# A first tile's products by kind behind 8 warm-up products, and the first head's outputs turned through HBM

## The chip, the cores and the metric

The kernel runs on one core of one Trainium2 chip. The metric is the device time of one execution in microseconds (us), lower is better. Three runs of the kernel before gave a median of 1380.77 us (1380.72 to 1381.59).

The core has five engines with a queue of instructions each, which run in order inside a queue and beside each other between queues: TensorE (PE, with its weight loads as PEld), VectorE (DVE), ScalarE (ACT), GpSimd (POOL) and SyncE (SP, which only starts DMA transfers here).

## The reference

Two layers on 512 tokens of width 1024. Each layer projects the normed x to pool inputs, q, k, v and two gates, mixes the tokens in two ways, adds the gated sum, and ends with a SwiGLU of width 2816.

```python
xn = rmsnorm(x, norm1_g[i])
u_pool, q, k, v, g_a, g_b = split(xn @ w_in[i])
q, k = rotary(rmsnorm(q, q_norm_g)), rotary(rmsnorm(k, k_norm_g))
# 4 heads; each has two q/k pairs of 128 and a v of 256; chunk-causal mask
p = softmax(q @ k.T * 128 ** -0.5)
o = (p[0] - lam * p[1]) @ v
o = rmsnorm(o, subln_g) * (1.0 - lam_init)
merged = sigmoid(g_a) * pool_mixer(u_pool) + sigmoid(g_b) * o
x = x + merged @ w_out[i]
gate, up = split(rmsnorm(x, norm2_g[i]) @ w_ffn_in[i])
x = x + (silu(gate) * up) @ w_ffn_out[i]
```

## The kernel before

**Products.** Every matrix product is made of three: an operand is split into a high part (a cast on ScalarE, `whi`, `xh`, `qh`, `ah`) and a low part (a subtraction on VectorE, `wlo`, `xl`, `ql`, `al`), and PE adds high times high, low times high and high times low into one PSUM bank. `split` (L214 to L216) does it for weights and activations alike; `product` (L304 to L315) issues the three.

**Order.** Python code issues the instructions. Work that has to wait for another engine is put off: `later` (L264) puts a function into a heap with a due time in a clock that counts columns of products issued (512 for a product of 512 columns), and `run_due` takes out what is due between two groups of three products. The framework's scheduler then orders every queue again, so that the program's order on an engine is not that of the code; names carry a number that grows with the order of the code, and the numbers of one tile differ a little between the two programs. Each buffer comes from a pool named by its tag: `mt` and `qn` have three buffers each, and a tile waits until one is free.

**Start (L406 to L485).** PE makes warm-up products of a zeroed tile `cold` (12, L406 to L408). `first_step(0)` (L450) loads the first weight piece and the first x tile in halves, splits the weights (L216), scales x by the norm's gain into `xh` on VectorE (L472) and makes `xl` (L473). `first_products` (L477) adds the products of one k into the four banks of `first_acc`, one for each 128 tokens: three products for a bank, then the next bank.

**Heads.** Heads come in the order 3, 2, 1, 0. The first head of layer 0 is treated apart (`at_start`). For each head, `attention` (L514) projects q and k for four token blocks t = 0 to 3. `evicted` (L625) takes the squares of a block out of PSUM into `qn` (L629), `rsqrt_mean` finds the norm's factor (VectorE L355, POOL L356), ScalarE scales the block (L634), VectorE rotates it (L385 to L393), and it is turned, so that `turn` (L527) can scale (L535) and split it into `qh` and `ql` (L216). `scores` (L539) makes the scores, their maxima and exponentials (L551); `turn_prob` (L568) splits the turned probabilities into `ah` and `al`; `weighted` (L587) multiplies them by v, takes squares into `mt` (L595) and a factor `r`; `gated` (L598, its instruction L599) scales `mt` with r and the gate `tb`; `turn_out` (L609) turns `mt` and puts it, scaled, into `mj` (L618). Then v and gate `tb` of the head are projected (`vh` L676, `tb` L679 and L680).

**Two ways to turn.** `turned` (L321) turns a tile through HBM: VectorE transposes blocks of 32 by 32 into `near` (L326), SP writes `near` to HBM (`away`, L327) and reads it back in four transfers (L331). For the first head, q, k, probabilities and outputs are instead transposed by PE against an identity (L317, L318).

**Merge.** For each head, `merged` (from L683) makes the pool mixer's input `up` (L699 to L710) and the gate `ta` (VectorE L733, tanh on ScalarE L737), and multiplies the pool part by its own weights `pw`. It follows a head by one: the merge of head 3 runs while head 2 is made, that of head 2 while head 1 is made.

## Time and profile before

| | before |
|---|---|
| median of three runs | 1380.77 us (1380.72 to 1381.59) |
| the profiled execution | 1380.28 us |
| its span, first to last instruction | 1378.5 us |
| chain that ended last: PE's share | 95% |
| mean granted TensorE clock | 0.999 |
| DMA, bytes moved | 224.07 MB, 163 GB/s |

The profile records one execution. Its "span" leaves out 1.8 us around the first and last instruction. A group's row reads: line, engine, operation, output and inputs with their shapes and count, then the busy time and the mean time of one in ns, then the idle time of the engine ahead of the group and what ended it. A row of the timeline reads: start and duration in us, engine, line, operation; in brackets stands the engine's idle time ahead of it and what released it. A matmul's row lasts longer than the distance to the next one, since matmuls are pipelined; what counts is the distance of the starts.

### The profile page before, as it was taken

The page shows a single profiled execution, that of the slowest core. Times are in us where ns is not written, and L with a number is a line of the kernel's source. Part 1 is how long each engine was busy: PE and PEld are TensorE (multiplying, and loading weights), DVE is VectorE, ACT ScalarE, POOL GpSimd, SP SyncE. Part 2 cuts the span into 40 slices and gives each one's busy share as a digit, 9 for nine tenths or more (in the row PEclk, how much of TensorE's full clock was granted, in tenths as well). Part 3 has the DMA queues.
Part 4 walks back from the last instruction along what each step waited for, and adds up shares of the span by engine and source line. Part 5 has one row for each costly group of instructions (what it writes and reads, how often), then busy time and mean ns, then how long its engine had stood idle before and what let it go on. Part 6 is the DMA issues. An engine that isn't in the chain of part 4 may idle for free.

```text
span 1378.5 us, 18671 instructions
## 1 busy us (share of the span) xinstructions
PE 1371.7 (100%) x6242; PEld 1138.8 (83%) x6242; DVE 995.6 (72%) x1787; ACT 774.9 (56%) x1577; POOL 129.2 (9%) x155
## 2 busy tenths in 40 slices
PE   9999999999999999999999999999999999999999
PEld 7888888888888888888888888888888888888887
DVE  7668677676968768678666696775878687686782
ACT  7675564554856545554367655545557665555540
POOL 3010100000101101110010001000001111000100
PEclk9999999999999999999999999999999999999999
DMA  8334454545668868686435454544536788787731
GB/s 312 99 130 126 129 152 141 150 123 153 126 188 194 226 186 222 172 204 189 144 108 150 122 186 134 164 124 138 172 111 139 194 212 219 187 212 179 204 122 61
DMA packets 141072, 224.07 MB, mean 163 GB/s; under 512 B 41392, under 2 KB 88496, under 8 KB 140976
## 3 DMA queue, kind: packets, MB, share of 16 engines
q1 hardware_dynamic: 130464, 187.20, 42.5%
q0 software_dynamic: 9216, 33.56, 14.2%
q10 hardware_dynamic: 1296, 2.13, 0.6%
q8 instruction: 49, 0.80, 0.2%
q14 instruction: 47, 0.39, 0.1%
HBM read 193.59 MB, written 29.23 MB: 162 GB/s over the span
## 4 chain that ended last, share of the span: by engine, by line
PE 95%; ACT 1%; DVE 1%; issue 1%; DMA 0%; POOL 0%; SPq 0%; ACTq 0%; DVEq 0%; POOLq 0%
PE mm L293 15%; PE mm L294 14%; PE mm L292 14%; PE mm L311 14%; PE mm L313 14%; PE mm L312 14%; PE sc L292 3%; PE sc L294 3%; PE sc L293 3%; PE sc L311 1%; PE sc L312 1%; ACT whi L216 1%; PE sc L313 1%; DVE wlo L216 0%; PE mm L318 0%
## 5 line engine op out<-in xcount | busy, mean ns | idle before, releaser
L216 DVE TENSOR_TENSOR wlo<-raw,whi 128x1024 fp32r<-128x1024 f32 (+1 forms) x221 | 267.6, 1215 | 74.9 <-ACT whi L216 74.0
L216 ACT CAST whi<-raw 128x1024 fp32r<-128x1024 f32 (+1 forms) x221 | 230.3, 1050 | 145.4 <-PE mm L294 57.8
L311 PE MATMUL mm<-whi,xh 128*128 128x512 f32 x480 | 188.9, 394 | 0.0
L313 PE MATMUL mm<-whi,xl 128*128 128x512 f32 x480 | 187.2, 390 | 0.0
L312 PE MATMUL mm<-wlo,xh 128*128 128x512 f32 x480 | 187.1, 390 | 0.0
L293 PE MATMUL mm<-fl,whi 128*128 128x512 f32 (+1 forms) x356 | 137.6, 387 | 0.0
L294 PE MATMUL mm<-fh,wlo 128*128 128x512 f32 (+1 forms) x356 | 137.6, 387 | 0.0
L292 PE MATMUL mm<-fh,whi 128*128 128x512 f32 (+1 forms) x356 | 137.6, 387 | 0.0
L752 DVE TENSOR_TENSOR res<-mm,res 128x512 f32<-128x512 f32 (+1 forms) x145 | 97.7, 679 | 45.0 <-PE mm L294 41.8
L242 POOL DMA_DIRECT2D wlo<-in_wts x64 | 56.1, 876 | 536.6 <-ACT wlo L241 342.8
L313 PEld LDWEIGHTS mm<-whi,xl 128*128 128x128 f32 x480 | 90.1, 188 | 19.2
L356 POOL TENSOR_TENSOR r<-r,mhalf 128x4 f32<-128x4 f32 (+1 forms) x64 | 57.4, 898 | 516.7 <-DVE r L355 503.0
L311 PEld LDWEIGHTS mm<-whi,xh 128*128 128x128 f32 x480 | 90.2, 188 | 17.3
L312 PEld LDWEIGHTS mm<-wlo,xh 128*128 128x128 f32 x480 | 90.3, 188 | 17.2
L311 PE MATMUL mm<-xh,whi 128*128 128x512 f32 x256 | 99.8, 390 | 0.0
L312 PE MATMUL mm<-xl,whi 128*128 128x512 f32 x256 | 99.8, 390 | 0.0
L313 PE MATMUL mm<-xh,wlo 128*128 128x512 f32 x256 | 99.6, 389 | 0.0
L292 PE MATMUL mm<-whi,xh 128*128 128x512 f32 x224 | 87.1, 389 | 0.0
L293 PE MATMUL mm<-wlo,xh 128*128 128x512 f32 x224 | 87.1, 389 | 0.0
L294 PE MATMUL mm<-whi,xl 128*128 128x512 f32 x224 | 87.1, 389 | 0.0
L241 ACT ACTIVATE wlo<-raw 128x1024 fp32r<-128x1024 f32 x64 | 67.7, 1058 | 29.5 <-PE mm L293 25.7
L292 PEld LDWEIGHTS mm<-fh,whi 128*128 128x128 f32 x356 | 66.9, 188 | 13.7
(232 smaller groups left out, 2964.2 us busy)
## 6 DMA issues: line engine op xcount, KB each, us to landing
raw<-in_wts SPq DMA_DIRECT2D x243, 512.0 KB, 3.9
wlo<-in_wts POOLq DMA_DIRECT2D x64, 512.0 KB, 6.3
away<-near SPq DMA_DIRECT2D x73, 256.0 KB, 2.2
near<-away SPq DMA_DIRECT2D x292, 64.0 KB, 2.5
away<-near SPq DMA_DIRECT2D x29, 128.0 KB, 1.7
near<-away SPq DMA_DIRECT2D x116, 32.0 KB, 2.5
pwr<-in_pool_w ACTq DMA_DIRECT2D x8, 256.0 KB, 3.1
out<-res SPq DMA_DIRECT2D x7, 256.0 KB, 2.0
```

Source lines behind the costliest of these rows:

```text
L216: return nc.scalar.copy(hi, src), nc.vector.tensor_sub(lo, src, hi.bitcast(F32))
L241: made[0] = nc.scalar.activation(lo, raw, AF.Copy, scale=-1.0)
L242: nc.gpsimd.dma_start(lo.rearrange("p a b -> p (a b)"), wts[piece_no], accum_op=ALU.add)
L292: nc.tensor.matmul(acc, lhsT=ah, rhs=bh, start=start, stop=False, **check)
L293: nc.tensor.matmul(acc, lhsT=ah, rhs=bl, start=False, stop=False, **check)
L294: last = nc.tensor.matmul(acc, lhsT=al, rhs=bh, start=False, stop=stop, **check)
L311: nc.tensor.matmul(acc, lhsT=ah, rhs=bh, start=i == 0, stop=False)
L312: nc.tensor.matmul(acc, lhsT=ah, rhs=bl, start=False, stop=False)
L313: last = nc.tensor.matmul(acc, lhsT=al, rhs=bh, start=False, stop=i == n - 1)
L356: nc.gpsimd.tensor_tensor(r, r, mhalf[:, :width], op=ALU.pow)
L752: return nc.vector.tensor_add(res[d][:, cs], acc, res[d][:, cs])
```

## The change

1. `WARM` goes from 12 to 8.
2. In `first_step(0)`, for the first half, only the cast to `whi` is issued ahead; the code issues the subtraction for `wlo` behind `xh` and `xl` of the first x tile.
3. The twelve products of the first x tile are issued by kind: high by high for four token blocks, then `xl` by `whi` for four, then `xh` by `wlo` for four.
4. The outputs of the first head go through `turned`, as those of the other heads do, with the delay `MERGE_AWAY`; the two constants of the other way go. Eight PE transposes of `mt` (two for each token block) go; four VectorE transposes, four writes to HBM and sixteen read-backs come. The HBM turn takes a second buffer of the tag `mt` for `near`.

```diff
-WARM = 12
+WARM = 8
...
-SCORE_WAIT, PROB_WAIT, AV_WAIT, NORM_WAIT, MERGE_WAIT = 33600, 25200, 11400, 15000, 15000
+SCORE_WAIT, PROB_WAIT, AV_WAIT = 33600, 25200, 11400
...
-                split(hi[:, ks, :], lo[:, ks, :], wr[:, ks, :])
+                if i or ks.start:
+                    split(hi[:, ks, :], lo[:, ks, :], wr[:, ks, :])
+                else:
+                    nc.scalar.copy(hi[:, 0, :], wr[:, 0, :])
...
                 made = nc.vector.scalar_tensor_tensor(xl[:, k, :], xr[:, a, :], g, xh[:, k, :].bitcast(F32), op0=ALU.mult, op1=ALU.subtract)
+                if not k:
+                    made = nc.vector.tensor_sub(lo[:, 0, :], wr[:, 0, :], hi[:, 0, :].bitcast(F32))
...
-    for step in steps[0] + steps[1]:
+    k, wh, wl = steps[0][0]
+    for a, b in ((xh, wh), (xl, wh), (xh, wl)):
+        for t in range(NT):
+            nc.tensor.matmul(first_acc[t], lhsT=a[:, 0, token(t)], rhs=b, start=a is xh and b is wh, stop=False)
+    clock[0] += 3 * NT * 512
+    for step in steps[0][1:] + steps[1]:
...
-                    if at_start:
-                        later(MERGE_WAIT - GATED, lambda: turn_out(t, m))
-                    else:
-                        near = turned(m, 2, "mt", 3)
-                        later(MERGE_AWAY - GATED, lambda: turn_out(t, near))
+                    near = turned(m, 2, "mt", 3)
+                    later(MERGE_AWAY - GATED, lambda: turn_out(t, near))
...
-                if at_start:
-                    tp = tr_ps()
-                    for a in range(2):
-                        transpose(tp[:, a * P:(a + 1) * P], m[:, a * P:(a + 1) * P])
-                    into, src = mj[:, :, token(t)], tp[:, :VD].rearrange("p (a c) -> p a c", a=2)
-                else:
-                    into, src = squares_of(mj[:, :, token(t)]), m
+                into, src = squares_of(mj[:, :, token(t)]), m
```

The change moves instructions on the queues in three places that matter below. The new file's lines differ from the old ones by a few (L595 is now L605, L216 stays).

The first place is VectorE's queue at the start of the program; before, it reads:

```order
L703 MEMSET us 128x16 x2
L216 TENSOR_TENSOR wlo<-raw_114,whi 128x512
L472 TENSOR_SCALAR xh<-res_82,scale 128x512
L473 SCALAR_TENSOR_TENSOR xl<-res_82,scale,xh 128x512
L216 TENSOR_TENSOR wlo<-raw_114,whi 128x512
```

And with the change:

```order
L704 MEMSET us 128x16 x2
L478 TENSOR_TENSOR wlo<-raw_110,whi 128x512
L475 TENSOR_SCALAR xh<-res_82,scale 128x512
L476 SCALAR_TENSOR_TENSOR xl<-res_82,scale,xh 128x512
L216 TENSOR_TENSOR wlo<-raw_110,whi 128x512
```

The subtraction for `wlo` has a new line, but it stands where it stood: the scheduler puts it ahead of `xh` and `xl` in both programs.

The second place is ScalarE's queue in the second head (j = 2) up to `qh` of its token block t = 1, here qh_662 made from near_872, later qh_658 made from near_884. Before, from the block's scaling back some rows:

```order
L634 ACTIVATE qn_917<-mm_807,r_923 128x128
L216 CAST whi_1016<-raw_1014 128x1024
L216 CAST whi_1022<-raw_1020 128x1024
L618 ACTIVATE mj_240<-mm_961,scale_70 128x128 x2
L535 ACTIVATE near_872<-near_872,scale_70 128x2x4x32
L629 ACTIVATE qn_988,ss4_989<-mm_927 128x128
L216 CAST qh_662<-near_872 128x4x128
```

With the change, where qn_932 is the q and k of block t = 2, qn_1000 that of t = 3, near_868 the first head's output t = 1 on its way through HBM, and pr_1081 the probabilities of t = 0:

```order
L635 ACTIVATE qn_932<-mm_803,r_938 128x128 x4
L630 ACTIVATE qn_1000,ss4_1001<-mm_942 128x128 x4
L635 ACTIVATE qn_1000<-mm_942,r_1006 128x128 x4
L561 ACTIVATE pr_1081,st_1082<-sc_1084,mx_1083 128x128
L561 ACTIVATE pr_1081,st_1082<-sc_1091,mx_1083 128x128
L677 ACTIVATE vh_1010<-mm_1038,stats_249 128x256
L619 ACTIVATE mj_236<-near_868,scale_70 128x128 x2
L568 ACTIVATE rc_1098<-st_1082 128x1
L680 ACTIVATE tb_1012<-mm_1038,stats_249 128x256
L681 ACTIVATE tb_1012<-tb_1012 128x256
L545 ACTIVATE near_884<-near_884,scale_70 128x2x4x32
L216 CAST qh_658<-near_884 128x4x128
```

`qh` of t = 1 stood ahead of all but the first square of block t = 3; now the whole eviction of t = 3, the exponentials of t = 0 and the first v and gate stand ahead of it.

The third place is ScalarE's queue at the end of the second head, where `ah` (ah_1483, later ah_1494) is the cast of the last block's probabilities and `mt` (mt_1511, later mt_1527) the squares of the weighted block t = 2. Before:

```order
L216 CAST whi_1606<-raw_1604 128x1024
L737 ACTIVATE ta_1490<-ta_1490 128x512
L216 CAST ah_1483<-pr_1296 128x512
L595 ACTIVATE mt_1511,sso_1510<-mm_1500 128x256
L216 CAST whi_1612<-raw_1610 128x1024
```

With the change:

```order
L216 CAST whi_1734<-raw_1732 128x1024
L605 ACTIVATE mt_1527,sso_1526<-mm_1516 128x256
L216 CAST whi_1789<-raw_1787 128x1024
L738 ACTIVATE ta_1561<-ta_1561 128x512
L216 CAST ah_1494<-pr_1312 128x512
```

And VectorE's queue at the same place with the change:

```order
L355 TENSOR_SCALAR r_1529<-sso_1526,rc_1237 128x1
L216 TENSOR_TENSOR wlo_1735<-raw_1732,whi_1734 128x1024
L609 SCALAR_TENSOR_TENSOR mt_1527<-mm_1516,r_1529,tb_1013 128x256
L734 TENSOR_TENSOR ta_1561<-mm_1508,hg_222 128x512
L216 TENSOR_TENSOR wlo_1790<-raw_1787,whi_1789 128x1024
```

`ah` stood ahead of `mt`; now it stands behind `mt` and behind the tanh of a gate tile `ta_1561`, which VectorE makes behind `mt`'s scaling. On PE, six products of 512 columns (mm_1508, which `ta_1561` is made from) stand between the weighted products of t = 2 (mm_1516) and the first one that reads `ah` (mm_1563); before, they were 18.

## The prediction

> **What bounds the kernel now.** I read the page's span and busy times first, then PE's waits.

> ```profile
> span 1378.5 us, 18671 instructions
> PE 1371.7 (100%) x6242; PEld 1138.8 (83%) x6242; DVE 995.6 (72%) x1787; ACT 774.9 (56%) x1577; POOL 129.2 (9%) x155
> ```
> ```profile
> PE sc L311 <- ACT pr L551: 1.6, 2, 1.0
> ```

> PE is busy for the whole span, and its longest wait behind the start is 1.6 us in two pieces. So time is won only where PE gets less work or the start is shorter, and lost wherever PE is made to wait: any wait on PE is added in full. The sum is made against the profiled execution, 1380.28 us (the span and 1.8 us around it); the median of the runs lies 0.5 us above.

> **The start (edits 1 to 3).**

> ```profile
> 1.59 0.15 PEld L408 LDWEIGHTS <-cold 128*128 128x128 bf16 x1 [0.28 <-issue]
> ...
> 4.57 0.15 PEld L408 LDWEIGHTS <-cold 128*128 128x128 bf16 x1 [0.27 <-issue]
> ...
> 4.78 0.48 DVE L472 TENSOR_SCALAR xh<-res,scale 128x512 fp32r<-128x512 f32 x1
> 4.97 0.31 PEld L408 LDWEIGHTS <-cold 128*128 128x128 bf16 x2 [0.24 <-issue]
> ...
> 5.40 0.19 PEld L480 LDWEIGHTS mm<-whi,xh 128*128 128x128 f32 x1
> ...
> 6.10 0.19 PEld L482 LDWEIGHTS mm<-whi,xl 128*128 128x128 f32 x1 [0.29 <-DVE xl L473]
> ...
> 6.21 0.19 PEld L480 LDWEIGHTS mm<-whi,xh 128*128 128x128 f32 x1
> 6.44 0.40 PE L480 MATMUL mm<-whi,xh 128*128 128x512 f32 x1
> ```

> By the rows of the order, VectorE does the same things in the same sequence as before, so `xh` still ends at 4.78 + 0.48 = 5.26. The first real weight load came at 5.40, behind the last warm-ups; without those it can come at 5.26 plus one handover of about 0.06, at 5.32. The third product waited for `xl` until 6.10; issued by kind, the first product that needs `xl` is the fifth. The load at 6.10 was followed by the next at 6.21, so a product starts 0.11 behind its load, and the fourth product started at 6.44. Now it can start at 5.32 + 0.11 + 3 x 0.229 = 6.12 (0.229 is the distance of products, below). That is **0.3 us gained**, and the load for `xl`, due at 6.12, just meets it. If VectorE did `xh` first, as the code is written, some 0.6 (the `wlo` subtraction) would come on top; the order rows exclude it. No DMA of the start moves.

> The eight warm-ups end early. Loads of warm-ups follow each other at (4.57 - 1.59) / 7 = 0.426 us and from 4.97 on closer: some 3.8 us behind the first product, at 1.18 by the same timeline, the pace rises. Eight of them end at 1.59 + 7 x 0.426 = 4.57, and PE then stands idle until 5.3. Whether the pace still rises is a rival, below; I take it that it does, since the hole is 0.7 of some 4 us.

> **Eight PE transposes (edit 4, what goes).**

> ```profile
> 77.49 0.38 PE L318 MATMUL mm<-ident,mt 128*128 128x128 f32 x2
> ...
> 77.95 0.39 PE L312 MATMUL mm<-wlo,xh 128*128 128x512 f32 x1
> ...
> 80.24 0.40 PE L313 MATMUL mm<-whi,xl 128*128 128x512 f32 x1
> ```

> From 77.95 to 80.24 there are ten distances of products: 0.229 each. From 77.49 to 77.95 a pair of transposes and one product pass: the pair costs 0.46 - 0.229 = 0.23, four pairs **0.9 us gained**.

> **The HBM turn (edit 4, what comes).** VectorE gets four transposes of 0.435 (row below), 1.7 us, at 72% busy. ScalarE's `mj` copies change only their source. SP gets four writes and sixteen read-backs:

> ```profile
> 79.75 0.34 SPq L327 DMA_DIRECT2D away<-near  x1
> 81.98 1.73 SPq L331 DMA_DIRECT2D near<-away  x4
> ```

> That is 4 x 2.07 = 8.3 us of SP's queue. Weights' loads and the read-back of the second head's q and k queue behind them. I cost that at nothing: `whi` casts in this stretch wait for no load (row below), and the read-back of `near` for t = 1 has over 3 us in hand by the chain below. Otherwise each 0.1 us of lateness there would add to A.

> What costs is the new order on ScalarE and VectorE. The schedule puts other work ahead of what PE waits for.

> **A: `qh` of t = 1 in the second head.** Before:

> ```profile
> 79.98 0.28 ACT L629 ACTIVATE qn<-mm 128x128 f32<-128x128 f32 x1
> ...
> 81.00 0.64 ACT L618 ACTIVATE mj<-mm,scale 128x128 f32<-128x128 f32 x2
> ...
> 87.65 0.68 ACT L216 CAST qh<-near 128x512 fp32r<-128x512 f32 x1
> ...
> 90.72 1.15 ACT L634 ACTIVATE qn<-mm,r 128x128 f32<-128x128 f32 x4 [0.67 <-POOL r L356]
> ...
> 93.92 0.37 ACT L551 ACTIVATE pr<-sc,mx 128x128 f32<-128x128 f32 x1 [0.66 <-DVE mx L550]
> ...
> 94.28 0.50 ACT L535 ACTIVATE near<-near,scale 128x256 f32<-128x256 f32 x1
> ...
> 96.28 0.42 ACT L680 ACTIVATE tb<-tb 128x256 f32<-128x256 f32 x1
> ```
> ```profile
> 96.93 0.28 PE L311 MATMUL sc<-qh 128*128 128x256 f32 x1
> ```
> ```profile
> 84.79 0.56 DVE L385 TENSOR_TENSOR m<-qn,hg 128x128 f32<-128x128 f32 x3 [2.89 <-ACT qn L634]
> ...
> 85.71 0.71 DVE L326 STREAM_TRANSPOSE near<-qn 128x512 f32<-128x512 f32 x1
> ```
> ```profile
> L216 DVE TENSOR_TENSOR wlo<-raw,whi 128x1024 fp32r<-128x1024 f32 x12 | 14.5, 1211 | 0.8 <-ACT whi L216 0.6
> L216 ACT CAST whi<-raw 128x1024 fp32r<-128x1024 f32 x12 | 12.5, 1060 | 0.2 <-PE mm L313 0.2
> ...
> L356 POOL TENSOR_TENSOR r<-r,mhalf 128x1 f32<-128x1 f32 x8 | 4.5, 560 | 56.0 <-DVE r L355 48.3 <-DVE up L698 6.8 <-DVE m L385 0.9
> L356 POOL TENSOR_TENSOR r<-r,mhalf 128x4 f32<-128x4 f32 x4 | 4.1, 1013 | 38.1 <-DVE r L355 38.1
> ...
> L595 ACT ACTIVATE mt<-mm 128x256 f32<-128x256 f32 x8 | 3.1, 393 | 6.1 <-PE mm L313 4.7 <-PE mm L318 1.5
> ...
> L595 ACT ACTIVATION_READ_ACCUMULATOR mt<-mm 128x1 f32 x8 | 1.7, 208 | 0.0
> L355 DVE TENSOR_SCALAR r<-sso,rc 128x1 f32<-128x1 f32 x8 | 1.6, 200 | 0.0
> ...
> L326 DVE STREAM_TRANSPOSE near<-mt 128x256 f32<-128x256 f32 x3 | 1.3, 435 | 0.0
> ```

> PE's clock starts at W = 77.49, the end of the last weighted block. Before, PE read this `qh` at 96.93, 19.4 behind W, and it had been cast nine us earlier. Now PE reaches it 19.2 behind W (three more products stand ahead, +0.7; four pairs fewer, -0.9).

> ScalarE's clock starts at E, the end of the squares of block t = 2. Nine products stand behind W (8 x 0.229, the last ends 0.40 later: 2.23), then four squares (81.00 - 79.98 = 1.02) and a `qh` cast (0.63) between them: E = W + 3.9, so PE needs the cast at E + 15.3. The chain from E, in the new order: one `whi` cast 1.06, two `wlo` 2.42, the new transpose of an output 0.44, another `wlo` 1.21, `r` on VectorE 0.20, on POOL first the output's 0.56 and then the block's 1.01, scaling 1.15 (row 90.72), rotation and transpose 1.63 (84.79 to 86.42), only then the squares of t = 3, 1.02, for which `qn` has no buffer before; `r` again 1.21, scaling 1.15, two exponentials 0.74 (94.28 - 93.92 for one), two `mj` copies 0.64, and v, scale, cast, `rc` and two `tb`, all of 94.28 to 96.70, 2.42. That makes 16.9, with six handovers of 0.06 17.2: PE waits **1.9 us**. One `wlo` of 1.21 more or less in the chain bounds it: 0.7 to 3.1. The output's read-back is no part of it: sent at E + 3.9, it lands by the rows of SP's queue some 6.2 later, at E + 10.1, and ScalarE takes it at E + 13.8. Queued behind the waiting ScalarE are only v and `tb`.

> **B: `ah` of t = 3, end of the second head.**

> ```profile
> L599 DVE SCALAR_TENSOR_TENSOR mt<-mm,r,tb 128x256 f32<-128x256 f32 x7 | 3.4, 484 | 3.9 <-POOL r L356 3.9
> ...
> L733 DVE TENSOR_TENSOR ta<-mm,hg 128x512 f32<-128x512 f32 x2 | 1.4, 680 | 0.0
> L737 ACT ACTIVATE ta<-ta 128x512 f32<-128x512 f32 x2 | 1.3, 631 | 0.7 <-DVE ta L733 0.7
> ```
> ```profile
> 132.46 0.60 ACT L216 CAST ah<-pr 128x512 fp32r<-128x512 f32 x1
> ```

> Behind the weighted block t = 2 PE has six products, 1.37 us, before it needs `ah`; it had 18. The cast stands behind this chain: the drain 0.16, squares and their read 0.39 + 0.21, `r` on VectorE 0.20, a `wlo` 1.21 (longer than POOL's 0.56 beside it), `mt`'s scaling 0.48, `ta` 0.68, tanh 0.63, the cast itself 0.60: 4.56. PE waits 4.56 - 1.37 = **3.2 us**. If VectorE is ahead of its `wlo`, the chain begins with `ta`, 0.17 behind the sixth product: 1.37 + 0.17 + 0.68 + 0.63 + 0.60 - 1.37 = 2.1. If the third product also waits for `al` behind another `wlo`, 3.6. `wlo` and `whi` casts that stand between feed later products and are not waited for.

> **C and smaller ones.**

> ```profile
> 105.71 0.29 DVE L216 TENSOR_TENSOR al<-pr,ah 128x128 fp32r<-128x128 f32 x1 [0.73 <-ACT ah L216]
> ```

> Here VectorE waited for `ah` and was at hand. Now `up` of head 3 (shape of the `ta` row, 0.68) stands ahead of this `al` in VectorE's order: 0.17 + 0.68 + 0.29 = 1.14 behind the last `up` product, and PE has two products of 256 columns (0.12 each) and one of 512 in that time, 0.47: **0.7 us**, with 0 below if VectorE gets it done in a gap. For other places where scores meet a later exponential I take 0.5 (0 to 1).

> **Sum**: 1380.3 - 0.3 - 0.9 + 1.9 + 3.2 + 0.7 + 0.5 = 1385.4 for the profiled execution's kind, rounded with the 0.5 to the median 1385.8. With all terms at their low ends 1382.4, with all at their high ends 1388.0. Behind the second head the two programs run in the same order, so what is lost there stays lost.

> **Rivals.**

> 1. *The pace rises late.* If it needs an unbroken stretch like the 3.8 us of before, counted from the first real product, products of 0.426 instead of 0.229 run for 3.8 us: 3.8 x (1 - 0.229 / 0.426) = 1.8 us on top, 1387.6. For it speaks that no row shows a rise after a hole; against, that PE is busy most of the time. Chance 0.18.

> [...]

> 2. *A and C are hidden, B is not*: 1380.8 - 1.2 + 3.2 + 0.5 = 1383.3, within 0.2%. ScalarE took `qh` at 87.65, nine us ahead, and may still be early if the POOL steps overlap. Chance 0.12.

> 3. *The other side: both chains hidden.* PE never waits at A or B and only the gains are left: 1380.8 - 1.2 = 1379.6. It decides at chain A under 15.3 and B under 1.4 us. For it: ScalarE is 56% busy. Against it: B's four serial steps from `ta` on alone take 2.1 more than PE has. Chance 0.07; nearly all of it within 0.2%.

> 4. *The stalls make others behind them*, through late `mj` or merge tiles, two more of B's lower size, 4.2: 1390.0. Chance 0.06.

> 5. *The code's order holds on VectorE*: 0.6 better than any of these; the order rows are against it. Chance 0.01.

> **How the numbers follow.** The forecast, A, B and C paid and the pace as before, has 0.56. 0.2% of the time, 2.8 us, is about what a measurement can tell from no change: slower begins at 1383.5, faster at 1378.0. The forecast and rivals 1 and 4 are slower, all but a tail of the forecast near 1383: 0.79. Rivals 2, 3 and the tail are within: 0.18. Faster: 0.03. The range 1382.4 to 1388.8 holds the forecast's bounds, most of rival 1 and 2, and leaves out 3 and 4.

> **What would show it.** In the start: the first real load at 5.32, the fourth product at 6.12 and no wait for `xl`; distances of 0.43 behind 5.3 would mean rival 1. No L318 rows of `mt`. Among PE's waits, one of about 2 us for ScalarE's `qh` (or `near`) near 97 us, one of about 3 us for `ah` near 140, one of 0.7 for VectorE's `al` near 117. From 145 us on each group of products should lie later by one constant amount, about 5. I am wrong if PE's waits sum to under 2 us there, if they lie elsewhere, or if weights' loads come late behind the new transfers on SP's queue.

## The result and the profile after

| | before | after |
|---|---|---|
| median of six runs | 1380.88 us | 1387.92 us (1387.29 to 1388.90) |
| the profiled execution | 1380.28 us | 1387.48 us |
| its span | 1378.5 us | 1385.6 us |
| chain that ended last: PE's share | 95% | 92% |

The changed kernel takes 1.0051 times as long, with an interval of 1.0041 to 1.0061: 7.0 us more. The forecast was 1385.8, slower, in a range of 1382.4 to 1388.8.

The page's first lines and PE's waits of the changed kernel:

```profile
span 1385.6 us, 18681 instructions
PE 1373.3 (99%) x6230; PEld 1138.4 (82%) x6230; DVE 997.8 (72%) x1791; ACT 775.8 (56%) x1577; POOL 130.4 (9%) x155
```
```profile
PE mm L311 <- ACT ah L216: 3.4, 2, 3.2
PE sc L311 <- ACT pr L561: 1.6, 2, 1.0
PE sc L311 <- ACT qh L216: 1.5, 1, 1.5
...
PE mm L313 <- DVE al L216: 0.5, 1, 0.5
PE mm L494 <- DVE xh L475: 0.5, 1, 0.5
```

The three forecast waits are there: `ah` 3.2 (B), `qh` 1.5 (A), `al` 0.5 (C). The wait on the exponentials was there before. But the waits' sum is not what the time rose by, and PE's busy time has grown by 1.6 us, though PE does less work. The timeline of PE shows it behind wait B:

```profile
137.66 0.39 PE L313 MATMUL mm<-xh,wlo 128*128 128x512 f32 x1
141.29 0.38 PE L311 MATMUL mm<-vh,ah 128*128 128x256 f32 x1 [3.24 <-ACT ah L216]
...
142.33 0.34 PE L313 MATMUL mm<-vh,al 128*128 128x256 f32 x1
142.47 0.42 PE L311 MATMUL mm<-vh,ah 128*128 128x256 f32 x1
142.68 0.41 PE L312 MATMUL mm<-vl,ah 128*128 128x256 f32 x1
...
145.24 0.63 PE L313 MATMUL mm<-uh,pw 128*128 128x512 f32 x1
145.67 0.46 PE L311 MATMUL mm<-uh,pw 128*128 128x512 f32 x1
145.97 0.40 PE L312 MATMUL mm<-ul,pw 128*128 128x512 f32 x1
```

Until 142.3 products follow each other as always; from 142.47 on, a product of 256 columns takes 0.213 instead of 0.118 and one of 512 columns 0.427 (145.24 to 145.67) instead of 0.227; from 145.97 on the old pace is back. The windows say why; the columns are the window, its sum, busy times and counts of PE, PEld, DVE, ACT and POOL, then the granted clock, the DMA share and GB/s:

```profile
141.30:142.30 1.00, 1.00 (x5) 0.89 (x6) 0.66 (x1) 0.53 (x2) 0.00 (x0) 1.00 0.00 0
142.30:145.90 3.60, 3.60 (x15) 3.28 (x14) 0.00 (x0) 0.00 (x0) 0.00 (x0) 0.53 0.00 0
145.90:150.00 4.10, 4.10 (x19) 3.35 (x19) 4.09 (x8) 2.01 (x6) 0.55 (x1) 1.00 0.46 116
```

The granted clock is 0.53 over 3.6 us, right behind a wait of 3.2 us; the trace's own record of it has 0.5 from 142.39 to 145.80, 3.4 us. In these 3.4 us PE gets (1 - 0.227 / 0.427) x 3.4 = 1.6 us less done. The span's rise of 7.1 us, by its terms:

| term | forecast | measured in the profile |
|---|---|---|
| start | -0.3 | +0.2: the squares of the first head's block t = 2 begin at 62.61, 62.40 before |
| eight PE transposes | -0.9 | -0.9 (taken over: they are gone) |
| A, `qh` at 97 | 1.9 | 1.7 |
| B, `ah` at 140 | 3.2 | 3.4 (141.29 - 137.66 less one product) |
| C, `al` at 117 | 0.7 | 0.7 |
| smaller waits | 0.5 | 0.4 (what is left of the 7.1; PE lost 0.3 of it ahead of a product at 114.30) |
| half clock behind B | 0 | 1.6 |
| sum | 5.1 | 7.1 |

The chain of B stands on ScalarE as drawn up in the forecast, squares, tanh, cast:

```profile
136.97 0.19 ACT L605 ACTIVATION_READ_ACCUMULATOR mt<-mm 128x1 f32 x1
...
140.09 0.63 ACT L738 ACTIVATE ta<-ta 128x512 f32<-128x512 f32 x1 [1.20 <-DVE ta L734]
140.63 0.60 ACT L216 CAST ah<-pr 128x512 fp32r<-128x512 f32 x1
```

And A's, where ScalarE stood still twice ahead of the squares of t = 3 and the cast of `qh` ended at 98.66:

```profile
88.36 1.14 ACT L635 ACTIVATE qn<-mm,r 128x128 f32<-128x128 f32 x4 [1.51 <-POOL r L356]
91.27 0.28 ACT L630 ACTIVATE qn<-mm 128x128 f32<-128x128 f32 x1 [1.76 <-DVE near L326]
...
98.04 0.62 ACT L216 CAST qh<-near 128x512 fp32r<-128x512 f32 x1
```

So there were two questions: whether the half clock really comes from the wait, and whether the loss lies in the HBM turn itself or in the order around it.

### The profile page after: what moved, and what is told of

Read it like the earlier page. It is cut to its first block, busy times and chain, and to the rows that moved or that the text cites. A ratio compares the mean times of both kernels' runs of the same rounds, so it can differ in the third digit from the quotient of the medians.

```text
span 1385.6 us, 18681 instructions
## 1 busy us (share of the span) xinstructions
PE 1373.3 (99%) x6230; PEld 1138.4 (82%) x6230; DVE 997.8 (72%) x1791; ACT 775.8 (56%) x1577; POOL 130.4 (9%) x155
## 4 chain that ended last, share of the span: by engine, by line
PE 92%; ACT 2%; DVE 2%; issue 1%; POOL 1%; DMA 1%; SPq 0%; DVEq 0%; ACTq 0%; POOLq 0%
PE mm L293 14%; PE mm L294 14%; PE mm L292 14%; PE mm L313 13%; PE mm L311 13%; PE mm L312 13%; PE sc L292 3%; PE sc L294 3%; PE sc L293 3%; ACT whi L216 1%; PE sc L311 1%; POOL r L356 1%; PE sc L312 1%; PE sc L313 1%; DVE wlo L216 1%
## 5 line engine op out<-in xcount | busy, mean ns | idle before, releaser
L216 DVE TENSOR_TENSOR wlo<-raw,whi 128x1024 fp32r<-128x1024 f32 (+1 forms) x220 | 266.9, 1218 | 76.7 <-ACT whi L216 76.1
L216 ACT CAST whi<-raw 128x1024 fp32r<-128x1024 f32 (+1 forms) x220 | 229.3, 1051 | 145.8 <-PE mm L294 61.9
L311 PE MATMUL mm<-whi,xh 128*128 128x512 f32 x480 | 188.5, 393 | 0.0
L313 PE MATMUL mm<-whi,xl 128*128 128x512 f32 x480 | 187.1, 390 | 0.0
L312 PE MATMUL mm<-wlo,xh 128*128 128x512 f32 x480 | 187.1, 390 | 0.0
L356 POOL TENSOR_TENSOR r<-r,mhalf 128x4 f32<-128x4 f32 (+1 forms) x64 | 59.7, 936 | 522.0 <-DVE r L355 515.1
L313 PEld LDWEIGHTS mm<-whi,xl 128*128 128x128 f32 x480 | 90.1, 188 | 19.0
L311 PEld LDWEIGHTS mm<-whi,xh 128*128 128x128 f32 x480 | 90.2, 188 | 17.4
L312 PEld LDWEIGHTS mm<-wlo,xh 128*128 128x128 f32 x480 | 90.2, 188 | 17.3
L312 PE MATMUL mm<-xl,whi 128*128 128x512 f32 x256 | 99.8, 390 | 0.0
L311 PE MATMUL mm<-xh,whi 128*128 128x512 f32 x256 | 99.8, 390 | 0.0
L313 PE MATMUL mm<-xh,wlo 128*128 128x512 f32 x256 | 99.6, 389 | 0.0
```

The source lines that it names most:

```text
L216: return nc.scalar.copy(hi, src), nc.vector.tensor_sub(lo, src, hi.bitcast(F32))
L311: nc.tensor.matmul(acc, lhsT=ah, rhs=bh, start=i == 0, stop=False)
L312: nc.tensor.matmul(acc, lhsT=ah, rhs=bl, start=False, stop=False)
L313: last = nc.tensor.matmul(acc, lhsT=al, rhs=bh, start=False, stop=i == n - 1)
L356: nc.gpsimd.tensor_tensor(r, r, mhalf[:, :width], op=ALU.pow)
```

## The experiments

All times are medians; the kernel before had 1380.96 us in its runs beside the first eight experiments and 1381.16 beside the last three.

### The parts apart

The first kernel has the start's edits alone; the second has the HBM turn alone.

```diff
# start only: the changed kernel, with the first head's outputs as before
-                    near = turned(m, 2, "mt", 3)
-                    later(MERGE_AWAY - GATED, lambda: turn_out(t, near))
+                    if at_start:
+                        later(MERGE_WAIT - GATED, lambda: turn_out(t, m))
+                    else:
+                        near = turned(m, 2, "mt", 3)
+                        later(MERGE_AWAY - GATED, lambda: turn_out(t, near))
...
# turn only: the kernel before, with the same lines the other way round
```

> Edits 1 to 3 alone; the first head's outputs are transposed by PE as before. Theory: the 7 us come from the HBM turn's new order, and the start gives next to nothing, since its end is set by when the first loads land: time within 0.5 us of the kernel before (1380.9), first squares of q and k (L629 in the old file) at 19.6 to 20.0 against 19.57 before and 19.98 with the whole change; no wait of PE on qh near 97 or on ah near 140. Rival, the prediction's own term: the start gains 0.3, first squares at 19.25, time 1380.6. Rival, late pace: products 0.43 apart behind 5.3 us and a time near 1382.6.

> Edit 4 alone, with 12 warm-ups and the start of before. Theory: all of the loss is here: 1387.9, with the waits at 97 (1.5 us), 117 (0.5) and 140 (3.2) and a stretch of some 3.3 us behind the last one in which products of 512 columns stand 0.43 apart and PEclk is about 0.6. Rival: eight warm-ups or the start take part in the loss: 1385 to 1387.

Start only: 1381.02 us, ratio 1.0000 (0.9991 to 1.0008); its profile has no wait on `qh` or `al`. Turn only: 1388.18 us, ratio 1.0051 (1.0038 to 1.0063), with the same three waits and a granted clock of 0.63 from 141.3 to 145.9. All of the loss is the turn's.

The start's 0.3 us did not arrive in the profile. In that of the start alone the fourth real product comes at 6.14, as the forecast's 6.12 had it, 0.3 ahead of the 6.44 of before; but the first squares of q and k begin at 20.05 there, at 19.57 before. First the rows of before, then those of the start alone:

```profile
5.36 0.62 ACT L216 CAST whi<-raw 128x512 fp32r<-128x512 f32 x1 [1.22 <-DMA raw<-in_wts]
...
19.57 0.28 ACT L629 ACTIVATE qn<-mm 128x128 f32<-128x128 f32 x1 [1.05 <-PE mm L482]
```
```profile
6.10 0.62 ACT L216 CAST whi<-raw 128x512 fp32r<-128x512 f32 x1 [2.00 <-DMA raw<-in_wts]
...
18.78 0.19 PEld L487 LDWEIGHTS mm<-whi,xl 128*128 128x128 f32 x1 [0.49 <-DVE xl L476]
...
19.51 0.19 PEld L487 LDWEIGHTS mm<-whi,xl 128*128 128x128 f32 x1 [0.20 <-DVE xl L476]
...
20.05 0.28 ACT L639 ACTIVATE qn<-mm 128x128 f32<-128x128 f32 x1 [0.63 <-PE mm L487]
```

The second half of the first weight piece landed at 6.10 here, and at 5.36 in the profile of before. In the start alone ScalarE from there, and VectorE from 9.44, work on the other seven k without a pause, and PE catches up with them: its weight loads wait for VectorE's `xl` three times, 1.0 us in all, the last two just ahead of the first squares. In the profile of before no load waits for `xl` behind 6.10; there PE's own stream of 60 products, from 5.43 on, ends the stage. So the earlier products of the new start ran into VectorE's chain. The landing itself varies from profile to profile, 5.0 to 6.7 us, with the old start as with the new one, and it alone does not set the end: the first squares come 14.0 to 15.2 us behind it in the nine of thirteen profiles in which PE's products reach their full pace by 6.2 us.

### Is the half clock the wait's doing?

Spare products, whose result nobody reads, fill the wait at B without changing it: 12 of them (2.7 us), and in a second kernel the wait itself is taken away by issuing `ah` and `al` first.

```diff
# fill: n = 12, later 5 and 2
+                    if not layer and j == ORDER[1] and t == NT - 1:
+                        spare = tr_ps()
+                        with tc.issue_after(gate_last[0].ins):
+                            for _ in range(n):
+                                extra = nc.tensor.matmul(spare, lhsT=xh[:, 0, token(0)], rhs=xh[:, 0, :], start=True, stop=True)
...
# ah first: the squares mt of t = 2, the last gate's ta and tanh, and weight casts there
+                with behind_ah(...):   # issued behind ah and al of t = 3
```

> The whole change, and 12 spare products of 512 columns (their result is not used) put on PE behind the six products ahead of the wait for ah near 140 us, 2.7 us of work in a wait of 3.2. Theory: the half pace behind that wait comes from PE having been idle for 3.2 us; with the hole filled the clock stays at 1.00 and products 0.23 apart, and though PE does 2.7 us more work the time falls by 1.8: 1386.1. Rival: the half pace has another cause in that stretch (what the products read, or the transfers then): it stays, and the time stays at 1387.9.

> The whole change, but ScalarE's cast ah of block t = 3 in the second head, and VectorE's al, are issued ahead of the squares mt of t = 2, of the gate's tanh and of the weight casts there. Theory: the wait of 3.2 us goes and with it the half pace, 3.4 + 1.8 = 5.2 us: 1382.7. Rival 1: only the wait goes and the half pace stays: 1384.5. Rival 2: other work becomes late in its place (the gate, or the weights of head 1) and the time stays above 1386.

With 12 spare products: 1386.41 us, 1.5 less than the changed kernel though PE has 2.7 us more to do. With `ah` first: 1383.22 us, 4.7 less. Windows of the stretch, first with spare products, then with `ah` first:

```profile
142.30:145.90 3.60, 3.42 (x21) 3.06 (x22) 1.11 (x4) 0.73 (x3) 0.00 (x0) 1.00 0.00 0
```
```profile
142.30:145.90 3.60, 3.60 (x18) 2.98 (x16) 3.60 (x8) 2.98 (x8) 0.92 (x1) 1.00 0.54 178
```

The clock stays at 1.00 in both, and not in these two executions alone: the mean granted clock was 1.000 in all five executions with spare products and all eleven with `ah` first, and 0.998 or 0.999 in all six of the changed kernel (3.4 us at half clock take 0.001 off the mean). The spare products leave everything else in place, so the hole is the cause and not what is multiplied there; the difference of 1.5 us is the price worked out above, and 4.7 is close to the whole wait's 3.4 + 1.6 = 5.0.

### How long a hole it takes

> The whole change, and 5 spare products (result not used) behind the six products ahead of the wait near 140 us: 1.1 us of work, so that PE is idle for 2.1 us instead of 3.2. Theory: the clock falls when a stretch of some 3.4 us was mostly idle; 2.1 of 3.4 idle is on the border, and the wait of 1.5 us near 97 did not do it, so I expect no half pace and 1386.1. Rival: any wait over 2 us does it, and the time stays at 1387.9.

> As the run with 5 spare products, with 2 of them: PE idle for 2.8 us. Theory: by the share of a 3.4 us stretch, 2.8 idle is enough, but only if the stretch falls well; half pace in some executions: 1386.1 to 1387.9. Rival, a fixed limit near 3 us: no half pace, 1386.1 in every run.

> The kernel with 5 spare products once more, for its profile: its first profile had the half pace behind a wait of 2.1 us, at 143.2 to 146.6, which is 39.0 and 40.0 times 3.41 us behind the rise of the pace at the start (10.1). Theory: the clock is looked at every 3.41 us, on a grid that each execution starts at another phase; so the same kernel may or may not show it, and where it does, its begin and end lie a whole number of 3.41 us behind the rise at the start. Rival: the kernel decides, the same stretch 143.2 to 146.6 again, wherever the rise at the start lies.

> The kernel with 2 spare products once more: its first profile had no half pace behind a wait of 2.8 us. Theory: chance by execution, as above; half pace in this one would show that the same kernel does both (time about 1388). Rival: the length or the place of the wait decides, and there is none again (about 1386.5).

| spare products | PE's wait left | granted clock from 141.3 to 145.9 | time |
|---|---|---|---|
| 12 | 0.5 | 1.00 | 1386.41 |
| 5 | 2.1 | 0.71 | 1388.39 |
| 5, again | 2.1 | 0.65 | 1388.28 (one run) |
| 2 | 2.8 | 1.00 | 1386.92 |
| 2, again | 2.8 | 0.67 | 1387.07 (one run) |
| 0 (the changed kernel) | 3.2 | 0.63 | 1387.92 |

The expectations for 5 and 2 products reckon with the idle share of a stretch of 3.4 us; what the runs show of such a stretch is the last column of the table of six profiles below. My expectation for 5 products failed: a hole of 2.1 us was enough in both profiles. It is not in every execution: of the four in the first row for 5 products three took 1388.2 to 1388.7 us at a mean granted clock of 0.998 or 0.999, and the fourth 1386.06 at 1.000. The kernel with 2 products shows both in its profiles: none of it in the first, half clock in the second.

```profile
141.63 0.38 PE L312 MATMUL mm<-vh,ah 128*128 128x256 f32 x1 [2.79 <-ACT ah L216]
141.86 0.28 PE L313 MATMUL mm<-vl,ah 128*128 128x256 f32 x1
141.97 0.39 PE L312 MATMUL mm<-uh,pw 128*128 128x512 f32 x1
142.20 0.40 PE L313 MATMUL mm<-ul,pw 128*128 128x512 f32 x1
```
```profile
141.21 0.58 PE L312 MATMUL mm<-vh,ah 128*128 128x256 f32 x1 [2.79 <-ACT ah L216]
141.59 0.42 PE L313 MATMUL mm<-vl,ah 128*128 128x256 f32 x1
141.81 0.63 PE L312 MATMUL mm<-uh,pw 128*128 128x512 f32 x1
```

Same kernel, same wait of 2.79 us; in the first block a product of 512 columns takes 0.23, in the second 0.43. So the length of the hole does not decide alone. Where the half clock came, its end stands in a fixed relation to the rise of the pace at the start of the same execution. The second profile with 5 products has the rise inside the product at 9.42 and the end inside that at 145.87:

```profile
145.66 0.41 PE L314 MATMUL mm<-vh,al 128*128 128x256 f32 x1
145.87 0.52 PE L312 MATMUL mm<-uh,pw 128*128 128x512 f32 x1
146.22 0.39 PE L313 MATMUL mm<-ul,pw 128*128 128x512 f32 x1
```

The product at 145.87 takes 0.35 to the next one, between 0.227 and 0.427, so it ran at half pace for 0.27 of it and the end is at 146.14; in the same way the rise is at 9.60. The trace also records when the granted clock changes, and has 146.12 and 9.59 there. By that record, over the six profiles with a wait of more than 2 us:

| | clock rises at the start | half clock | from the rise to its end | PE idle in the 3.41 us ahead of it |
|---|---|---|---|---|
| the changed kernel | 5.86 | 142.39 to 145.80 | 139.95 | 2.3 |
| turn only | 4.77 | 141.30 to 144.71 | 139.95 | 3.1 |
| 5 products | 10.11 | 143.23 to 146.64 | 136.53 | 2.1 |
| 5 products, again | 9.59 | 142.71 to 146.12 | 136.53 | 2.1 |
| 2 products, again | 4.38 | 140.91 to 144.33 | 139.95 | 2.5 |
| 2 products | 4.20 | none | - | 1.9 and 0.9 by the estimate below, no half clock behind |

The two differences are themselves 3.41 us apart, the length of the half clock (142.39 to 145.80), and they are 41 and 40 times 3.413. From these numbers alone an estimate: within one execution the half clock begins and ends a whole number of 3.41 us behind the rise at the start. Why, no run shows, and no experiment moved these places.

Ahead of the five half clocks PE idled for 2.1 to 3.1 us of 3.41. In the first profile with 2 products the estimate puts one of the places at 4.20 + 136.53 = 140.73, inside the wait that begins at 138.84 and ends at 141.63, so that 1.9 us of it lie ahead and 0.9 behind; by the estimate that is why this execution escaped. No experiment varied the idling of such a stretch by itself; the nearest two of the six profiles are 2.1 us, followed by the half clock, and these 1.9 us, not followed by it. Behind the wait of 1.5 us at A the granted clock was 1.00 in all eight profiles that have it.

### Is it the turn or the order?

The HBM turn alone, with the start of before, and three places held in order by hand.

```diff
# qh, ql of t = 1 in the second head: made earlier, and ahead of the squares of t = 3
-  ... (17400 + 5700 * t if at_start else QK_AWAY) - NORMED - ROTATED
+  ... (17400 + 5700 * t if at_start else (18000 if not layer and j == ORDER[1] and t == 1 else QK_AWAY)) - NORMED - ROTATED
+                    if not layer and j == ORDER[1] and t == NT - 1:
+                        for x in halves_of[layer, j, "q", 1]:
+                            behind.enter_context(tc.issue_after(x.ins))
# al of t = 0 ahead of head 3's up
+                if not layer and j == ORDER[0] and not c:
+                    behind.enter_context(tc.issue_after(halves_of[layer, ORDER[1], 0][1].ins))
# ah, al of t = 3: as in the kernel with ah first
```

> Edit 4 alone (start of before, 12 warm-ups), with the order set by hand at the three places: qh and ql of t = 1 in the second head are issued earlier and ahead of the squares of t = 3, al of t = 0 ahead of head 3's up, ah and al of t = 3 ahead of the squares mt of t = 2. Theory: all of the loss is the order on ScalarE and VectorE, and the HBM turn itself costs nothing: 1380.9 - 0.9 (transposes) and up to 0.6 of small waits, 1380.0 to 1380.6, no wait of PE over 0.5 us between 70 and 146 us. Rival: the sixteen read-backs and four transposes cost by themselves (SP's queue, VectorE): waits come up elsewhere, 1382 or more.

1380.26 us, ratio 0.9994 (0.9985 to 1.0003): 7.9 us less than the same turn without the order. PE's waits in its profile:

```profile
PE sc L321 <- ACT pr L561: 1.6, 2, 1.0
PE mm L418 <- DVE us L713: 1.2, 1, 1.2
PE mm L450 <- DVE sq L446: 0.6, 1, 0.6
PE mm L321 <- ACT ah L216: 0.2, 1, 0.2
```

Those on `qh` and `al` are gone, the last is the 0.2 of before. The four transposes on VectorE and the twenty transfers cost PE nothing that shows; the order cost it.

### VectorE in the order of the code

```diff
# start only, and:
                 if not k:
-                    made = nc.vector.tensor_sub(lo[:, 0, :], wr[:, 0, :], hi[:, 0, :].bitcast(F32))
+                    with tc.issue_after(made.ins):
+                        made = nc.vector.tensor_sub(lo[:, 0, :], wr[:, 0, :], hi[:, 0, :].bitcast(F32))
```

> Edits 1 to 3 with the PE transposes of before, and VectorE held to the order in which the code is written: xh, xl, then wlo of the first half. Theory: the first real product comes 0.6 earlier (at 4.7) and the hole behind the warm-ups closes, but the first squares of q and k still come 14.2 us behind ScalarE's cast of the second half's weights, whose load lands when it lands: 1380.9 within 0.4, first squares at 19.5 to 20.2. Rival, as the prediction priced it: the 0.6 is kept: 1380.2, first squares at 19.0.

1380.56 us, ratio 0.9998 (0.9989 to 1.0006). The first real product comes at 4.99, 0.4 ahead of before, and the first squares begin at 20.53, 15.2 behind the cast at 5.37: in this profile the early products bring nothing to the end of the stage. The run misses the expected 14.2 by a microsecond: here `xh` of the second half waited for its load of x until 7.07.

### All of it in order

Edits 1 to 3 with `xh` first, and the ordered turn.

> The whole change with the order set by hand at all places: VectorE makes xh and xl ahead of wlo, and the three orders of the turn run. Theory: the start gives nothing that a time can show, the turn 0.7: 1380.0 to 1380.6, against 1380.26 for the ordered turn alone, so 0.5 under the kernel before and hardly to be told from it. Rival: the two parts add up, 1379.7 or less.

1379.45 us, ratio 0.9986 (0.9977 to 0.9995), the rival's figure and not mine. It is the one kernel of the study whose interval lies below the kernel before: 1.7 us under it in the same session, and 8.5 under the changed one. That the start adds to the ordered turn is not shown, since the two intervals overlap; in its profile the rise of the pace comes early, as a sign why it could:

```profile
4.94 0.70 PE L505 MATMUL mm<-whi,xh 128*128 128x512 f32 x2 [0.16 <-DVE xh L485]
5.49 0.62 PE L505 MATMUL sc<-whi,xh 128*128 128x512 f32 x2
```

### Eight warm-ups and the rise of the pace

Thirteen profiles share three starts. With 8 warm-ups and `wlo` first, four of eight show the late rise of the forecast's first rival; the kernel with 12 spare products is one of them:

```profile
6.51 1.05 PE L495 MATMUL sc<-whi,xh 128*128 128x512 f32 x2
7.37 1.05 PE L495 MATMUL mm<-whi,xl 128*128 128x512 f32 x2
...
9.93 0.73 PE L495 MATMUL sc<-wlo,xh 128*128 128x512 f32 x2
10.49 0.39 PE L486 MATMUL mm<-whi,xh 128*128 128x512 f32 x1
```

Two products take 0.86 until 9.9 us, then 0.23 each. The squares of the first head's block t = 2 begin at 63.5 to 63.8 in these four and at 62.4 to 62.9 in the other four: a late rise costs 1.0 us. With 12 warm-ups (three profiles) and with `xh` first (two), where PE has no hole or one of 0.2 us behind the warm-ups, the rise never came later than 6.2. The length of the hole does not decide it alone: the two longest, 0.85 and 0.87 (the kernel with 2 products), are not among the four; there the clock had risen at 4.38 and 4.20, ahead of the hole. What decides was not shown. The profile of the changed kernel happened to be an early one. Its six runs lie in two groups, 1387.3 to 1387.5 and 1388.4 to 1388.9, as a late rise in three of them would give; that is argued and not shown, since those runs have no profile.

## Why the prediction came out as it did

**The direction and the main terms were right.** That any wait on PE is paid in full, and that the order on ScalarE and VectorE would make them, held: taking away the order while the turn stays takes away the loss. B was forecast at 3.2 and measured at 3.4, by the chain as worked out (one link was another: `mt`'s scaling waited 0.4 us longer for POOL's `r` than for the `wlo` of 1.21 that was reckoned there). A was 1.9 against 1.7: its chain, from the first weight cast at 81.59 to the end of the `qh` cast at 98.66, took 17.1 us where 17.2 were reckoned. C was right at 0.7. The rivals 2 and 3, hidden chains, did not happen.

**The step that failed in size** is the sum's first sentence, "any wait on PE is added in full", taken as the whole price. A wait of 3.2 us cost 3.4 and then 1.6 more through the clock. The forecast weighed the clock for the start alone (rival 1) and not for the waits that it put into the middle of the run itself. With that term the forecast is 1387.4.

**The start's 0.3** was worked out rightly for the first products and wrongly for the stage. The fourth product did come at 6.14 to 6.34 in the four profiles with an early rise (6.8 to 6.9 in the other four). That it met 6.12 is in part luck: in the profile of before a product starts 0.03 behind its load (5.40 and 5.43), not 0.11, and in that of the start alone the first two distances take 0.54, not 0.46. But with the new start PE then waits for VectorE's `xl` of the later k, 0.5 to 1.3 us at its weight loads in those four profiles, and the gain is gone by the first squares. The times neither show a gain of 0.3 nor exclude it (start alone, 0.9991 to 1.0008 of the kernel before, some 1.2 us either way). What was missing beside the term is the late rise as a loss of 1.0 in a part of the executions. Rival 1 was priced at 1.8 and a chance of 0.18; it came in four of eight profiles, for 1.0.

**The order of the code on VectorE** was not kept, as the order rows said. Forced, it is worth at most what a time can hardly tell (1380.56 against 1381.02 for the start alone).

**SP's queue and VectorE's transposes** were put at nothing, and the ordered turn shows no cost of them: no wait on PE that was not there before, and a time within what was expected of it.

The median of 1387.92 lies inside the range; of the 2.1 us that it lies above the forecast, 1.6 are the half clock and 0.5 the start, by the terms of the profiled execution. (The sum's 1385.4 and the 0.5 make 1385.9; the forecast has 1385.8.)

## What to carry to other kernels

Where PE is busy all the time, as here (100% of the span before), a removed instruction is worth its own time and no more (0.9 us for the eight transposes), but a wait that a new order makes is worth its length and, as behind the wait of 3.2 us here, 1.6 us more while the clock is low: look at the granted clock of the window behind a long wait before the waits are summed. When a step moves to other queues, read the order of the built program at the places where PE waits next, and pin what PE waits for ahead of what it does not. A gain at the first instruction of a stage counts only if that stage ends on the same chain.
